# First-phase tiles in another order in memory, three pieces of work moved, and the last sums in fp32

## The chip, the cores and the metric

The kernel runs on one core of a Trainium2 chip. The metric is the device time of one execution in microseconds. Five engines work side by side, each through its own list of instructions in order: TensorE (PE; its weight loads are PEld), VectorE (DVE), ScalarE (ACT), GpSimd (POOL) and SyncE (SP), which here issues all transfers between HBM and on-chip memory. Semaphores tie the lists together. The matrix sums are built in PSUM, all other on-chip data are in SBUF.

## The reference

One layer over 2048 tokens of 1024 channels, in fp32. `gmlp_mixer` and `mlstm_mixer` are two groups of heads on the projections of the normed input; the rest is:

```python
h = rms_norm(x, g_mix)
proj = h @ w_in                                  # 1024 -> u, v, qk, vm, o, gates
gm = gmlp_mixer(u, v, ...)
ml = mlstm_mixer(q, k, vm, ig, fg, o, ...)       # chunks of 128, 4 heads
x = x + concat(gm, ml) @ w_out
h = rms_norm(x, g_ffn)
a, b = split(causal_dwconv(h @ w_up))            # 1024 -> 2 x 2816
x = x + (silu(a) * b) @ w_down
gate = sigmoid(rms_norm(x, g_ple) @ w_ple_gate)
x = x + gate * (p @ w_ple)                       # p: 2048 x 256
out = rms_norm(x, g_final)
```

## The kernel before

The tokens are cut into four blocks of 512. Every product is made of fp32r matmuls on values split into a high and a low part (`whi`/`wlo` for weights, `hh`/`hl` for data): high by high, high by low, low by high, 128 channels at a time. That is why each weight tile, once loaded (`wst`), needs a cast and a subtraction before TensorE can use it: `wsplit` (L102 to L111), with three buffers of each kind in `wpool`.

Phase 1 (`with mx`) runs block by block. `tok_group(0)` to `tok_group(3)` (matmuls in L325 to L327) make the token-major projections with four weight tiles each; then come the q/k tiles, the heads, and `w_out`, whose eight output tiles get the residual added on VectorE (L631) and are stored to HBM as `x1s` (L632). In blocks 1 to 3, `pend[1]`, which is `make_h`, makes the FFN inputs of the block before: it loads `x1s` back (L641), scales with the norm (L204) and stores the `td` tiles (L207). It is called between the layer norm of `gv` (`BN_STATS` L431, GpSimd's power L435, scaling L437) and `tok_group(3)`.

The FFN phase (`with fx`) takes the tokens in two halves. `up_half` makes, for 22 column blocks j, seven products (Winograd's form of a 2x2 block product; L762 to L764) from tiles T (`tt`, split in L680/L681 from `hx` loads) and combined weights (`sw`, split in L686/L687 from `wr`, loaded in L727 to L729). `down_half` sums over the 22 blocks in four double banks of PSUM (L848 to L850), adds the residual (L856), stores `x2s`, and sums squares (L141, L143, `st1` L148/L150). `Steps.run` writes out the matmul steps in order, each with its preparations some steps ahead. The FFN's buffers are slots of one pool, laid over the memory that phase 1 gave free: `w` for weights, `x` for loads, `k` for T tiles, `r` for split weights, `f` and `m`. PSUM is `banks`: four slots of two banks.

Last comes the gate (`Ple`), block by block: for each d of 8 output tiles, 24 matmuls of the gate (`ps`, lines L118, L119, L121 of `mm3`), six of `p @ w_ple` (`pp`), and then L915 (product with the norm `rB`), sigmoid L916, L917 and L918. The norm of a block's input, `n3[b]`, has steps: `st2a` (column sums by matmul L159/L160, the diagonal read out in L163, GpSimd's power), `st2b` (diagonals `dg`, L178) and `st3` (L184/L185 spread the norm over partitions, L187 copies it to SBUF). For block 0, `st2b` and `st3` stand between `steps.run()` and the gate. The last block is gated in two halves a and b of 256 tokens; their final norms go through the same steps, and `emit_half` multiplies (L961; some tiles on GpSimd) and stores (L962) tile by tile.

A scheduler keeps the written order on each engine nearly, but lets ready work of lower rank go between; which slot a tile gets is fixed when the program is built. All transfers are on SP in order, so one that waits holds up all behind it.

Of the kernel before, what the change touches and what calls it, by code (L numbers as in the profile page):

```python
# [41 lines left out]
def trunk_kernel(ctx: ExitStack, tc: tile.TileContext, xT, pT, w_u, w_qk, w_v0, w_v1,  # L42
# [6 lines left out]
    rpool = ctx.enter_context(tc.tile_pool(name="rpool", bufs=2))  # L49
    dram = ctx.enter_context(tc.tile_pool(name="dram", bufs=1, space=bass.MemoryType.DRAM))  # L50
    mx = ExitStack()
    wpool = mx.enter_context(tc.tile_pool(name="wpool", bufs=3))
    hpool = mx.enter_context(tc.tile_pool(name="hpool", bufs=2))
    xpool = mx.enter_context(tc.tile_pool(name="xpool", bufs=2))
    pacc = mx.enter_context(tc.tile_pool(name="pacc", bufs=5, space=PSUM))
    pm = mx.enter_context(tc.tile_pool(name="pm", bufs=3, space=PSUM))
    banks = None
# [20 lines left out]

    col = const.tile([P, NCOL], F32, name="col")
    DMA.dma_start(col, cols)  # L80

    def c1(i):
        return col[:, i:i + 1]
# [15 lines left out]
    one = const.tile([P, 1], F32, name="one")  # L99
    G.memset(one, 1.0)  # L100

    def wsplit(src, n, eng=None, leng=None):  # L102
        st = wpool.tile([P, 1024], F32, tag="wst", name="wst")
        DMA.dma_start(st[:, :n], src)
        hi = wpool.tile([P, 1024], F32R, tag="whi", name="whi")
        if eng is None:
            A.activation(hi[:, :n], st[:, :n], AF.Copy)  # L107
        else:
            eng.tensor_copy(hi[:, :n], st[:, :n])  # L109
        lo = wpool.tile([P, 1024], F32R, tag="wlo", name="wlo")  # L110
        (leng or V).tensor_tensor(lo[:, :n], st[:, :n], hi[:, :n].bitcast(F32), ALU.subtract)  # L111
        return hi, lo
# [19 lines left out]
    class SumSq:  # L132
# [36 lines left out]
        def st2b(self):  # L169
# [7 lines left out]
            for v, dg in zip((rh, rl), self.dg):  # L177
                V.tensor_tensor(dg.rearrange("p (c t) -> p c t", t=128), idb,  # L178
                                v.bitcast(F32).rearrange("p (c o) -> p c o", o=1).broadcast_to([P, nt, 128]),
                                ALU.mult)  # L180

        def st3(self):
            bp = pmt()[:, :self.n]
            PE.matmul(bp, onesr, self.dg[0], start=True, stop=False)  # L184
            PE.matmul(bp, onesr, self.dg[1], start=False, stop=True)  # L185
            self.rB = rpool.tile([P, TB], F32, tag="rB", name="rB")[:, :self.n]
            A.activation(self.rB, bp, AF.Copy)  # L187
# [33 lines left out]
        DMA.dma_start(t[4][:, kk, :], t4)  # L221

    with mx:
        big = mx.enter_context(tc.tile_pool(name="mbig", bufs=1))
        tp = mx.enter_context(tc.tile_pool(name="mtmp", bufs=2))
        sm = mx.enter_context(tc.tile_pool(name="msmall", bufs=2))

# [9 lines left out]
        for k0, k1 in ((0, 1), (1, 2), (2, 4), (4, 6), (6, 8)):  # L237
            xs = xpool.tile([P, 2, TB], F32, tag="xs", name="xs")
            DMA.dma_start(xs[:, 0:k1 - k0, :], xT[0, :, k0:k1, :])
            for k in range(k0, k1):  # L240
                ysplit(xs[:, k - k0, :], C_GMIX, k, h)
                nq.add(xs[:, k - k0, :])
            if k0 == 0:
                w_first = wsplit(w_v0[0], 2 * GW[0], V, V)
        nq.st1()

        ws = big.tile([P, 8, 128], F32, name="ws")
# [51 lines left out]
        for b in range(NB):  # L299
# [135 lines left out]
            G.tensor_tensor(lrs, lrs, mhalf, ALU.pow)  # L435
            for t in range(CPB):
                V.tensor_scalar(gv[:, t, :], gv[:, t, :], mu[:, t, 0:1], lrs[:, t:t + 1], ALU.subtract, ALU.mult)  # L437
            if b:
                pend[1]()
            ps = tok_group(3)  # L440
            for t in range(CPB):
                evac(osig[:, t, 128:512], ps[t][:, 0:384], t)
            for t in range(CPB):
                A.activation(osig[:, t, :], osig[:, t, :], AF.Sigmoid)
            if b == 0:
# [201 lines left out]
    with ExitStack() as fx:  # L647
# [231 lines left out]

        class Ple:  # L880
            def __init__(self, i):
                self.i, self.x, self.h = i, [], []

            def start(self, ds=range(KD)):
                i = self.i
                for d in ds:
                    if i % 2 == 0:
                        x = load2(x2s[i][:, d, :], "xg")
                    else:
                        if d % 2 == 0:  # L890
                            self.xp = pairs(slot("f", "xg"))
                            DMA.dma_start(self.xp, x2s[i][:, d:d + 2, :])
                        x = self.xp[:, d % 2, :]
                    h = slot("k", "hg", F32R)
                    A.activation(h[:, :TB], x, AF.Copy, scale=c1(C_GPLE + d))
                    V.scalar_tensor_tensor(h[:, TB:], x, c1(C_GPLE + d), h[:, :TB].bitcast(F32), ALU.mult, ALU.subtract)
                    self.x.append(x)
                    self.h.append(h)
# [8 lines left out]

            def out_tile(self, d, si, ps):
                lo, hi = self.segs[si]
                pp = acc()[:, :hi - lo]  # L910
                mm3(pp, [(wpe[k][0][:, d * 128:(d + 1) * 128], wpe[k][1][:, d * 128:(d + 1) * 128],
                          self.p[0][:, k * TB + lo:k * TB + hi], self.p[1][:, k * TB + lo:k * TB + hi]) for k in range(2)])
                gs = slot("m", "gs")[:, :hi - lo]
                x = self.x[d][:, lo:hi]
                V.tensor_tensor(gs, ps, n3[self.i].rB[:, lo:hi], ALU.mult)  # L915
                A.activation(gs, gs, AF.Sigmoid)  # L916
                V.tensor_tensor(gs, gs, pp, ALU.mult)  # L917
                V.tensor_tensor(x, x, gs, ALU.add)  # L918
                f = self.fins[si]
                f.add(x)  # L920
                if len(self.segs) > 1:
                    tc.keep_in_program_order(A.activation(x, x, AF.Copy, scale=c1(C_GFIN + d)))
                if d == KD - 1:
                    f.st1()

            def run(self, hooks, cut=(0, TB)):
# [4 lines left out]
                for t in range(KD + len(segs) - 1):  # L931
                    for si, (lo, hi) in enumerate(segs):
                        d = t - si
                        if not 0 <= d < KD:
                            continue
                        w = wpg[d]
                        ps = acc()[:, :hi - lo]
                        mm3(ps, [(w[0][:, k * 128:(k + 1) * 128], w[1][:, k * 128:(k + 1) * 128],
                                  self.h[k][:, lo:hi], self.h[k][:, TB + lo:TB + hi]) for k in range(KD)])
                        if si == 0:  # L940
                            for fn in hooks.get(d, ()):
# [2 lines left out]
                        while len(last) > lag and t > 1:  # L944
                            self.out_tile(*last.pop(0))
                        if len(segs) > 1 and (d, si) == (KD - 2, 1):
                            self.fins[0].st2()
                for o in last:
                    self.out_tile(*o)
                return self.fins  # L950
# [4 lines left out]
                V.scalar_tensor_tensor(x, x, c1(C_GFIN + k), fin.rB, ALU.mult, ALU.mult)  # L955
                DMA.dma_start(out[o.i, :, k, :], x)

        def emit_half(o, fin, lo, hi, pool):
            for k in (pool + tuple(k for k in range(KD) if k not in pool)):
                x = o.x[k][:, lo:hi]  # L960
                (G if k in pool else V).tensor_tensor(x, x, fin.rB, ALU.mult)  # L961
                DMA.dma_start(out[o.i, :, k, lo:hi], x)  # L962

        ple = [Ple(b) for b in range(NB)]

# [33 lines left out]
        ex = {}  # L999
        for b in range(2):  # L1000
            at(1 + b, 5, lambda b=b: n3[b].st2a(r3[:, b, :]))
        up_half(1, ex)

        ex = {}
# [8 lines left out]
        down_half(1, ex)  # L1013
        steps.run()

        n3[0].st2b()
        n3[0].st3()
        wpe.extend(split4(w_pe[k], "r") for k in range(2))
        fin = None
        for b in range(NB):  # L1020
# [14 lines left out]
                continue  # L1035
            cut = (0, TB // 2, TB)
            fa, fb = ple[b].run(hooks, cut)
            fa.st3()
            fb.st2()
            emit_half(ple[b], fa, 0, TB // 2, (0, 4))  # L1040
            fb.st3()
            emit_half(ple[b], fb, TB // 2, TB, (2,))


def _pack(x, p, g_mix, w_in, gm_ln_g, gm_ln_b, gm_ws, gm_bs, ml_conv_w, ml_conv_b, ml_b_i, ml_b_f, ml_norm_g,
# [47 lines left out]
```

## Time and profile before

| | |
|---|---|
| median of 3 runs | 2482.81 us (2481.03 to 2486.6) |
| profiled execution | 2480.78 us |
| its span, first to last instruction | 2479.0 us |
| TensorE busy | 2404.0 us (97%) |
| VectorE, ScalarE, GpSimd busy | 1697.2 (68%), 1066.4 (43%), 53.5 us (2%) |
| mean granted TensorE clock | 0.99 |
| DMA | 324.99 MB, mean 131 GB/s |

The sum of busy time says that TensorE sets the time; what else there is must be found in the places where it waits. A wait is put down to the engine and line that ended it last.

### The profile page before, as it was taken

What the parts mean: (1) busy time and instruction counts of PE and PEld (TensorE: products, weight loads), DVE (VectorE), ACT (ScalarE), POOL (GpSimd) and SP (SyncE); (2) the same over time, 40 slices, a digit from 0 to 9 for tenths busy, and PEclk for the clock granted to TensorE, in tenths of its full rate; (3) what the DMA queues carried; (4) which work ended last, traced back from release to release, by engine and by line L of the source; (5) the groups of instructions that cost most, each with busy time, mean ns of one, the idle gap of its engine ahead of it and who ended that gap; (6) DMA issues with size and microseconds to landing.
All of it is one profiled execution on the core that took longest, in us unless ns stands there. A gap on an engine that the chain in (4) does not pass through costs nothing.

```text
span 2479.0 us, 30740 instructions
## 1 busy us (share of the span) xinstructions
PE 2404.0 (97%) x11596; PEld 2039.9 (82%) x11596; DVE 1697.2 (68%) x2846; ACT 1066.4 (43%) x1707; POOL 53.5 (2%) x62
## 2 busy tenths in 40 slices
PE   8999999999999979999999999999999999989997
PEld 8888987988898858888888887788888888868887
DVE  7687667688656578888776343878877746354666
ACT  3453364256236355444455332444444435332223
POOL 1000000000000000000000000000000000000000
PEclk9999999999999989999999999999999999999999
DMA  6326424472542262344227474322222266550221
GB/s 200 96 69 213 153 85 135 151 241 70 175 132 86 94 238 77 112 157 157 94 91 258 140 250 136 120 77 77 86 93 77 97 212 206 184 189 13 68 69 68
DMA packets 125173, 324.99 MB, mean 131 GB/s; under 512 B 13664, under 2 KB 15840, under 8 KB 125024
## 3 DMA queue, kind: packets, MB, share of 16 engines
q1 hardware_dynamic: 125024, 323.02, 39.3%
q8 instruction: 91, 1.49, 0.2%
q14 instruction: 58, 0.48, 0.1%
HBM read 260.05 MB, written 62.91 MB: 130 GB/s over the span
## 4 chain that ended last, share of the span: by engine, by line
PE 89%; DVE 5%; DMA 3%; ACT 2%; issue 1%; POOL 1%; SPq 0%; DVEq 0%; POOLq 0%; ACTq 0%
PE ub L764 6%; PE ub L763 6%; PE ub L762 6%; PE dn L848 6%; PE dn L849 6%; PE dn L850 6%; PE ua L764 5%; PE ua L762 5%; PE ua L763 5%; PE acc L118 4%; PE acc L119 4%; PE acc L121 4%; PE bank L118 3%; PE bank L119 3%; PE bank L121 3%; PE acc L326 3%
## 5 line engine op out<-in xcount | busy, mean ns | idle before, releaser
L762 PE MATMUL ub<-tt,sw 128*128 128x512 f32 x704 | 276.1, 392 | 13.2 <-ACT tt L680 11.6
L848 PE MATMUL dn<-at,wd 128*128 128x512 f32 x704 | 274.1, 390 | 5.0 <-ACT wd L686 3.3
L763 PE MATMUL ub<-tt,sw 128*128 128x512 f32 x704 | 275.7, 392 | 1.3 <-DVE tt L681 1.3
L764 PE MATMUL ub<-tt,sw 128*128 128x512 f32 x704 | 275.4, 391 | 0.5 <-DVE sw L687 0.5
L849 PE MATMUL dn<-at,wd 128*128 128x512 f32 x704 | 273.9, 389 | 0.0
L850 PE MATMUL dn<-at,wd 128*128 128x512 f32 x704 | 272.5, 389 | 0.0
L686 ACT ACTIVATE sw<-wr 128x1024 fp32r<-128x1024 f32 x132 | 140.3, 1063 | 289.2 <-PE ua L763 257.6
L687 DVE TENSOR_TENSOR wd<-wd 128x1024 fp32r<-128x1024 f32 x88 | 107.9, 1226 | 198.4 <-ACT wd L686 195.1
L687 DVE TENSOR_TENSOR sw<-wr,sw 128x1024 fp32r<-128x1024 f32 x132 | 161.4, 1223 | 75.7 <-ACT sw L686 75.6
L762 PE MATMUL ua<-tt,sw 128*128 128x512 f32 x528 | 205.7, 390 | 0.7 <-ACT sn L768 0.7
L763 PE MATMUL ua<-tt,sw 128*128 128x512 f32 x528 | 205.5, 389 | 0.0
L764 PE MATMUL ua<-tt,sw 128*128 128x512 f32 x528 | 205.4, 389 | 0.0
L111 DVE TENSOR_TENSOR wlo<-wst,whi 128x1024 fp32r<-128x1024 f32 (+2 forms) x144 | 158.6, 1105 | 52.5 <-ACT whi L107 31.2
L326 PE MATMUL acc<-wlo,hh 128*128 128x384 f32 (+1 forms) x512 | 175.6, 343 | 7.8 <-DVE wlo L111 7.8
L325 PE MATMUL acc<-whi,hh 128*128 128x384 f32 (+1 forms) x512 | 172.6, 342 | 8.2 <-DVE whi L109 7.7
L686 ACT ACTIVATE wd<-wd 128x1024 fp32r<-128x1024 f32 x88 | 93.2, 1059 | 192.5 <-PE dn L849 187.4
L327 PE MATMUL acc<-whi,hl 128*128 128x384 f32 (+1 forms) x512 | 174.7, 341 | 0.0
L762 PEld LDWEIGHTS ub<-tt,sw 128*128 128x128 f32 x704 | 133.1, 189 | 42.6 <-ACT tt L680 12.7
L848 PEld LDWEIGHTS dn<-at,wd 128*128 128x128 f32 x704 | 132.1, 188 | 34.5 <-ACT wd L686 4.5
L763 PEld LDWEIGHTS ub<-tt,sw 128*128 128x128 f32 x704 | 133.1, 189 | 30.2 <-DVE tt L681 2.4
L764 PEld LDWEIGHTS ub<-tt,sw 128*128 128x128 f32 x704 | 133.1, 189 | 28.3 <-DVE sw L687 0.9
L850 PEld LDWEIGHTS dn<-at,wd 128*128 128x128 f32 x704 | 132.2, 188 | 27.8 <-DVE wd L687 0.2
(296 smaller groups left out, 5073.9 us busy)
## 6 DMA issues: line engine op xcount, KB each, us to landing
wd<-w_down SPq DMA_DIRECT2D x88, 512.0 KB, 3.6
wr<-w_up SPq DMA_DIRECT2D x44, 512.0 KB, 3.6
wr<-w_up SPq DMA_DIRECT2D x88, 256.0 KB, 4.4
act<-fc SPq DMA_DIRECT2D x44, 512.0 KB, 4.0
wd<-act SPq DMA_DIRECT2D x88, 256.0 KB, 3.9
wst<-w_v SPq DMA_DIRECT2D x48, 384.0 KB, 3.2
wst<-w_qk SPq DMA_DIRECT2D x32, 512.0 KB, 3.6
wst<-w_out SPq DMA_DIRECT2D x32, 512.0 KB, 3.5
```

What stands on the lines that cost most here:

```text
L118: PE.matmul(ps, wh, mh, start=(i == 0), stop=False)
L119: PE.matmul(ps, wh, ml, start=False, stop=False)
L326: PE.matmul(ps[t][:, :n], a_h, rl, start=False, stop=False)
L327: PE.matmul(ps[t][:, :n], a_l, rh, start=False, stop=(k == KD - 1))
L686: A.activation(hi, x, AF.Copy)
L687: V.tensor_tensor(lo, x, hi.bitcast(F32), ALU.subtract)
L762: PE.matmul(ps, hi[:, c], t[:, :HALF], start=first, stop=False, skip_group_check=on)
L763: PE.matmul(ps, hi[:, c], t[:, HALF:], start=False, stop=False, skip_group_check=on)
L764: PE.matmul(ps, lo[:, c], t[:, :HALF], start=False, stop=last, skip_group_check=on)
L848: PE.matmul(ps, hi[:, c], t[:, :HALF], start=(j == 0), stop=False)
L849: PE.matmul(ps, hi[:, c], t[:, HALF:], start=False, stop=False)
L850: PE.matmul(ps, lo[:, c], t[:, :HALF], start=False, stop=(j == NJ - 1))
```

## The change

The diff has six parts. The pools of phase 1 are opened in another order, so that other tiles lie where the FFN's first slots will be. The first weight tile is loaded at the top over ScalarE's queue. `pend[1]()` is called after `tok_group(3)`. `n3[0].st2b` and `st3` become early work of `up_half(1)`, block 3. In the gate, `ps` and `pp` are the two banks of one slot (`gt`). At the end, the two half norms are made by `q1` (plain fp32 matmuls of one column each over the sum of squares) and `q2` (one fp32 diagonal, one fp32 matmul over `ones`), the result is read straight from PSUM by VectorE alone, and two tiles go out in one transfer.

```diff
-    wpool = mx.enter_context(tc.tile_pool(name="wpool", bufs=3))
+    big = mx.enter_context(tc.tile_pool(name="mbig", bufs=1))
     hpool = ...
     xpool = ...
+    wpool = mx.enter_context(tc.tile_pool(name="wpool", bufs=3))
...
     DMA.dma_start(col, cols)
+    w_raw = wpool.tile([P, 1024], F32, tag="wst", name="wst")
+    A.dma_start(w_raw[:, :2 * GW[0]], w_v0[0])
...
+        def q1(self):
+            mp = pmt()
+            nt = self.n // 128
+            for c in range(nt):
+                PE.matmul(mp[:, c:c + 1], self.a[:, c * 128:(c + 1) * 128], one, start=True, stop=True)
+            r = rpool.tile([P, CPB], F32, tag="nr", name="nr")[:, :nt]
+            V.tensor_scalar(r, mp[:, :nt], 1.0 / D, EPS, ALU.mult, ALU.add)
+            G.tensor_tensor(r, r, mhalf[:, :nt], ALU.pow)
+            self.r = r
+        def q2(self):
+            nt = self.n // 128
+            dg = self.t("dgf")
+            V.tensor_tensor(dg..., ident..., self.r..., ALU.mult)
+            bp = pmt()[:, :self.n]
+            PE.matmul(bp, ones, dg, start=True, stop=True)
+            self.rB = bp
...
-                w_first = wsplit(w_v0[0], 2 * GW[0], V, V)
+                w_first = wsplit(None, 2 * GW[0], V, V, w_raw)
...
-            if b:
-                pend[1]()
             ps = tok_group(3)
             for t in range(CPB):
                 evac(osig[:, t, 128:512], ps[t][:, 0:384], t)
+            if b:
+                pend[1]()
...
-                pp = acc()[:, :hi - lo]
+                ps, pp = ps[:, 0, :hi - lo], ps[:, 1, :hi - lo]
...
-                        ps = acc()[:, :hi - lo]
+                        ps = bank2("gt")
...
-                            self.fins[0].st2()
+                            self.fins[0].q1()
...
-        def emit_half(o, fin, lo, hi, pool):
-            for k in (pool + tuple(k for k in range(KD) if k not in pool)):
-                x = o.x[k][:, lo:hi]
-                (G if k in pool else V).tensor_tensor(x, x, fin.rB, ALU.mult)
-                DMA.dma_start(out[o.i, :, k, lo:hi], x)
+        def emit_half(o, fin, lo, hi):
+            for k in range(0, KD, 2):
+                for i in range(2):
+                    x = o.x[k + i][:, lo:hi]
+                    V.tensor_tensor(x, x, fin.rB, ALU.mult)
+                DMA.dma_start(out[o.i, :, k:k + 2, lo:hi], o.xp[k // 2][:, :, lo:hi])
...
+        at(3, 5, n3[0].st2b)
+        at(3, 3, n3[0].st3)
         up_half(1, ex)
...
-        n3[0].st2b()
-        n3[0].st3()
         wpe.extend(split4(w_pe[k], "r") for k in range(2))
...
-            fa.st3()
-            fb.st2()
-            emit_half(ple[b], fa, 0, TB // 2, (0, 4))
-            fb.st3()
-            emit_half(ple[b], fb, TB // 2, TB, (2,))
+            fa.q2()
+            fb.q1()
+            emit_half(ple[b], fa, 0, TB // 2)
+            fb.q2()
+            emit_half(ple[b], fb, TB // 2, TB)
```

VectorE at the end of block 1's `tok_group(2)`, before the change (`xs` is `make_h`'s, `gv` and `mu` the layer norm's, `whi` and `wlo` the weights of `tok_group(3)`):

```order
L204 SCALAR_TENSOR_TENSOR xs<-xs,col,rB 128x512
L432 BN_AGGR mu<-bnst 128x2
L204 SCALAR_TENSOR_TENSOR xs<-xs,col,rB 128x512
L434 TENSOR_SCALAR lrs<-mu 128x4
L109 CAST whi<-wst 128x768
L437 TENSOR_SCALAR gv<-gv,mu,lrs 128x512 x4
L111 TENSOR_TENSOR wlo<-wst,whi 128x768
L109 CAST whi<-wst 128x768
L111 TENSOR_TENSOR wlo<-wst,whi 128x768
```

The same place in the changed kernel (its lines L113 and L115 are the cast and the remainder, L229 is `make_h`, L455 to L461 the layer norm):

```order
L113 CAST whi<-wst 128x768
L455 BN_STATS bnst<-gv 128x6
L115 TENSOR_TENSOR wlo<-wst,whi 128x768
L456 BN_AGGR mu<-bnst 128x2
L455 BN_STATS bnst<-gv 128x6 x2
L456 BN_AGGR mu<-bnst 128x2
L229 SCALAR_TENSOR_TENSOR xs<-xs,col,rB 128x512
L456 BN_AGGR mu<-bnst 128x2
L455 BN_STATS bnst<-gv 128x6
L113 CAST whi<-wst 128x768
L456 BN_AGGR mu<-bnst 128x2
L229 SCALAR_TENSOR_TENSOR xs<-xs,col,rB 128x512
```

The two remaining weight tiles moved up past most of `make_h` and past the `gv` scaling; in the changed kernel the last `wlo` stands directly ahead of L461.

SP at the step from phase 1 to the FFN, before the change (`x1s` the last stores of phase 1, `wr` the first up weights, `hx` the T tiles' data):

```order
L630 DMA xr<-xT 128x512
L632 DMA x1s_81<-xr 128x512 x2
L727 DMA wr<-w_up 128x1024
L728 DMA wr<-w_up 128x512
L729 DMA wr<-w_up 128x512
L675 DMA hx<-td_1_86 128x512 x4
```

And in the changed kernel:

```order
L654 DMA xr<-xT 128x512
L656 DMA x1s_84<-xr 128x512 x2
L751 DMA wr<-w_up 128x1024
L752 DMA wr<-w_up 128x512
L753 DMA wr<-w_up 128x512
L699 DMA hx<-td_1_89 128x512 x4
```

Nothing moved here: the loads stand behind the same two stores.

TensorE at the step from the FFN to the gate, before the change (`dn` are the down sums, `dg` the norm's diagonals, `hg` and `wg` the gate's data and weights):

```order
L848 MATMUL dn<-at,wd 128x512
L849 MATMUL dn<-at,wd 128x512
L850 MATMUL dn<-at,wd 128x512
L184 MATMUL bank<-dg,onesr 128x512
L185 MATMUL bank<-dg,onesr 128x512
L118 MATMUL bank<-hg,wg 128x512
L119 MATMUL bank<-hg,wg 128x512
```

And in the changed kernel:

```order
L872 MATMUL dn<-at,wd 128x512
L873 MATMUL dn<-at,wd 128x512
L874 MATMUL dn<-at,wd 128x512
L122 MATMUL gt<-hg,wg 128x512
L123 MATMUL gt<-hg,wg 128x512
```

The two matmuls of the norm are gone from between the down sums and the gate.

## Rows read from the trace of the kernel before

**Rows 1.** The page, part 1: engine, busy us, share of the span, instructions.
```profile
PE 2404.0 (97%) x11596; PEld 2039.9 (82%) x11596; DVE 1697.2 (68%) x2846; ACT 1066.4 (43%) x1707; POOL 53.5 (2%) x62
```

**Rows 2.** TensorE's waits, whole span: us in total, times, longest us.
```profile
PE bank L184 <- DVE dg L178: 12.0, 2, 9.6
PE ub L762 <- ACT tt L680: 11.6, 2, 9.0
...
PE bank L118 <- DVE junk L163: 1.1, 1, 1.1
```

**Rows 3.** TensorE's timeline, first matmul: start us, us, instruction, idle before, releaser.
```profile
6.73 1.32 PE L325 MATMUL acc<-whi,hh 128*128 128x392 f32 x3 [6.73 <-DVE whi L109]
```

**Rows 4.** VectorE's timeline, 5 to 7 us.
```profile
5.35 0.75 DVE L191 SCALAR_TENSOR_TENSOR hl<-xs,col,hh 128x512 fp32r<-128x512 f32 x1 [3.68 <-ACT hh L190]
6.02 0.56 DVE L109 CAST whi<-wst 128x784 fp32r<-128x784 f32 x1
```

**Rows 5.** TensorE's waits from 284 to 300, 505 to 515, 715 to 735 us.
```profile
PE acc L326 <- DVE wlo L111: 2.2, 1, 2.2
...
PE acc L326 <- DVE wlo L111: 2.3, 1, 2.3
...
PE acc L326 <- DVE wlo L111: 2.7, 1, 2.7
PE acc L325 <- DVE whi L109: 0.8, 1, 0.8
```

**Rows 6.** VectorE's timeline, 293 to 297 us.
```profile
293.64 1.91 DVE L437 TENSOR_SCALAR gv<-gv,mu,lrs 128x512 f32<-128x512 f32 x4 [0.90 <-POOL lrs L435]
295.47 0.95 DVE L111 TENSOR_TENSOR wlo<-wst,whi 128x768 fp32r<-128x768 f32 x1
```

**Rows 7.** SP's timeline, 866 to 873 us (issues).
```profile
866.99 5.76 SPq L632 DMA_DIRECT2D x1s<-xr  x2
872.85 0.38 SPq L727 DMA_DIRECT2D wr<-w_up  x1
```

**Rows 8.** ScalarE's timeline at 878 us.
```profile
877.99 1.06 ACT L686 ACTIVATE sw<-wr 128x1024 fp32r<-128x1024 f32 x1 [23.35 <-DMA wr<-w_up]
```

**Rows 9.** TensorE's timeline, 2215 to 2235 us.
```profile
2215.78 0.39 PE L850 MATMUL dn<-at,wd 128*128 128x512 f32 x1
...
2218.50 0.39 PE L850 MATMUL dn<-at,wd 128*128 128x512 f32 x1
...
2229.63 0.63 PE L118 MATMUL bank<-hg,wg 128*128 128x512 f32 x1
...
2234.75 0.44 PE L118 MATMUL bank<-hg,wg 128*128 128x512 f32 x1
```

**Rows 10.** VectorE's timeline at 2215 us.
```profile
2215.50 3.48 DVE L856 TENSOR_TENSOR xr<-xr,dn 128x1024 f32<-128x1024 f32 x3
```

**Rows 11.** Windows: length, busy PE, PEld, DVE, ACT, POOL, granted clock, DMA share, GB/s.
```profile
2220.00:2230.00 10.00, 1.48 (x3) 1.12 (x4) 9.16 (x13) 4.51 (x8) 0.00 (x0) 0.56 0.98 352
2230.00:2240.00 10.00, 10.00 (x35) 7.99 (x34) 2.77 (x5) 2.97 (x4) 0.00 (x0) 0.76 0.31 126
```

**Rows 12.** TensorE's timeline at 2461 us.
```profile
2461.61 0.40 PE L121 MATMUL bank<-pp,wg 128*128 128x256 f32 x2
```

**Rows 13.** VectorE's timeline, 2457 to 2475 us.
```profile
2457.50 0.42 DVE L915 TENSOR_TENSOR gs<-bank,rB 128x256 f32<-128x256 f32 x1
...
2459.77 0.43 DVE L143 TENSOR_TENSOR sq<-sq 128x256 f32<-128x256 f32 x1
...
2465.11 0.75 DVE L961 TENSOR_TENSOR xg<-xg,rB 128x256 f32<-128x256 f32 x2
...
2471.79 2.96 DVE L961 TENSOR_TENSOR xg<-xg,rB 128x256 f32<-128x256 f32 x7 [1.09 <-ACT rB L187]
```

**Rows 14.** SP's timeline, 2462 to 2479 us (issues).
```profile
2464.07 12.51 SPq L962 DMA_DIRECT2D out<-xg  x16
```

**Rows 15.** TensorE's timeline at 37 us (L363 is an fp32 matmul, four per block).
```profile
37.41 0.95 PE L363 MATMUL pm<-one,gpad 128*128 128x1 f32 x8
```

More of the change, by code (lines that the diff above doesn't have):

```diff
@@ L100, in trunk_kernel, with wsplit @@
     G.memset(one, 1.0)
-    def wsplit(src, n, eng=None, leng=None):
-        st = wpool.tile([P, 1024], F32, tag="wst", name="wst")
-        DMA.dma_start(st[:, :n], src)
+    def wsplit(src, n, eng=None, leng=None, st=None):
+        if st is None:
+            st = wpool.tile([P, 1024], F32, tag="wst", name="wst")
+            DMA.dma_start(st[:, :n], src)
         hi = wpool.tile([P, 1024], F32R, tag="whi", name="whi")
@@ L180, in st2b @@
                                 ALU.mult)
+        def q1(self):
[10 more added lines that the diff above has]
+            dg = self.t("dgf")
+            V.tensor_tensor(dg.rearrange("p (c t) -> p c t", t=128),
+                            ident.rearrange("p (o t) -> p o t", o=1).broadcast_to([P, nt, 128]),
+                            self.r.rearrange("p (c o) -> p c o", o=1).broadcast_to([P, nt, 128]), ALU.mult)
+            bp = pmt()[:, :self.n]
+            PE.matmul(bp, ones, dg, start=True, stop=True)
+            self.rB = bp
         def st3(self):
@@ L223, in trunk_kernel @@
     with mx:
-        big = mx.enter_context(tc.tile_pool(name="mbig", bufs=1))
         tp = mx.enter_context(tc.tile_pool(name="mtmp", bufs=2))
@@ L881, in __init__ @@
             def __init__(self, i):
-                self.i, self.x, self.h = i, [], []
+                self.i, self.x, self.xp, self.h = i, [], [], []
             def start(self, ds=range(KD)):
@@ L890, in start @@
                         if d % 2 == 0:
-                            self.xp = pairs(slot("f", "xg"))
-                            DMA.dma_start(self.xp, x2s[i][:, d:d + 2, :])
-                        x = self.xp[:, d % 2, :]
+                            self.xp.append(pairs(slot("f", "xg")))
+                            DMA.dma_start(self.xp[-1], x2s[i][:, d:d + 2, :])
+                        x = self.xp[-1][:, d % 2, :]
                     h = slot("k", "hg", F32R)
@@ L922, in out_tile @@
                     tc.keep_in_program_order(A.activation(x, x, AF.Copy, scale=c1(C_GFIN + d)))
-                if d == KD - 1:
+                if d == KD - 1 and len(self.segs) == 1:
                     f.st1()
@@ L936, in run @@
                         w = wpg[d]
-                        ps = acc()[:, :hi - lo]
-                        mm3(ps, [(w[0][:, k * 128:(k + 1) * 128], w[1][:, k * 128:(k + 1) * 128],
+                        ps = bank2("gt")
+                        mm3(ps[:, 0, :hi - lo], [(w[0][:, k * 128:(k + 1) * 128], w[1][:, k * 128:(k + 1) * 128],
                                   self.h[k][:, lo:hi], self.h[k][:, TB + lo:TB + hi]) for k in range(KD)])
```

## The prediction, made before the changed kernel had run

> **What bounds the kernel now.** I read the page's engine shares first, then TensorE's waits, then the timelines at the places the change touches. TensorE is busy for 2404.0 of 2479.0 us [rows 1], so nothing that only relieves another engine counts. What can be won are the 75 us in which TensorE waits, and the few places where its clock is low. The list of its waits [rows 2] has four that the change touches: the start; the weight splits of the last token group in blocks 1 to 3; the step from phase 1 to the FFN; and the step from the FFN to the gate. The sum of squares at the very end adds a tail in which TensorE has nothing left to do.
>
> The sum is made against the profiled execution, 2480.78 us (span 2479.0, 1.78 around it). The median of the runs is 2482.81, 2.03 above it; I add that at the end.
>
> **Start.** The first matmul starts at 6.73 us and waits for the cast of the weight tile [rows 3]. That cast stands on VectorE behind `hl` (0.75 us at 5.35) and starts at 6.02 [rows 4]. After the change the weight tile is requested from ScalarE's queue, before SP has issued its other loads, and its cast and its remainder stand ahead of `hl`. The first matmul then needs `hh`, which is ready just as `hl` starts, at 5.35, so at most 6.73 - 5.35 = 1.4 us go. The second and later tiles come over the same queue as before, and a wait for them can take it back. I take -1.0, range 0 to -1.4.
>
> **Phase 1, last token group.** In blocks 1, 2 and 3 the split weights of `tok_group(3)` come late: 2.2, 2.3 and 2.7 + 0.8 us [rows 5], 8.0 in all. The reason is on VectorE [rows 6]: 0.90 us in which it waits for GpSimd's power, then 1.91 us of `gv` scaling, and only at 295.47 the remainder `wlo` for which TensorE stands still until 296.4. Ahead of these stand four scalings of `make_h` (L204). The order of the changed kernel puts the cast and remainder of the third weight tile ahead of `make_h` and among the `BN_STATS`, and those of the fourth ahead of the `gv` scaling. By the same durations, the third remainder is ready at about 288, when TensorE wants it at 296.4 - 2.2 = 294.2; the fourth can start when the first weight tile is used up, two weight tiles earlier than it is wanted. So all of it goes: -8.0. What is late next are the `wlo` of the next `w_qk` tiles, which VectorE now makes after two more L204: these are wanted only in the last third of a tile of 24 matmuls. SP now issues the stores of `make_h` later, between the `w_qk` and `w_u` loads; the loads of the second `w_qk` tile and of `w_u` stood behind such stores before. From below: if one of the two remainders of each block is still late, half stays. Range -4 to -8.
>
> **Layout of the first tiles.** TensorE's last `w_out` matmul ends near 871.7 and the FFN then waits 9.0 us and more [rows 2]. The chain is on SP: the last `x1s` store is issued after VectorE has added the residual (SP's row of two stores, 866.99 and 5.76 long, ends at 872.75), then at 872.85 the first `w_up` load [rows 7], and ScalarE can split it at 877.99, having waited 23.35 us for just that load [rows 8]. The new layout lets the `w_up` tile lie over memory that is free long before. But the order shows both loads and the `hx` loads still behind that last store on SP. What held SP was the store, not the memory. I take 0. From above: if the load could start with the earlier store, at 866.99, 5.9 us would go. From below: the FFN's `k` and `r` slots now lie over the last weight tiles, whose matmuls end at 871.7, while the data to be written there arrive at 877.99; that costs nothing until the load becomes 6 us earlier.
>
> **FFN to gate.** Twelve down matmuls take 2218.50 - 2215.78 = 2.72 us, 0.227 each; the last starts at 2218.50, so the next could at 2218.73. L184 waits 9.6 us [rows 2], and the first gate matmul starts at 2229.63 [rows 9]. It is the order: the norm of gate block 0 (`st2b`, `st3`) stands after `steps.run()`, so L178 is behind the whole residual and squares of the last down block. After the change this norm is made in `up_half(1)`, before the whole of `down_half(1)`, and the gate's matmuls follow the last down matmul in TensorE's order. They need only bank 0 of the down sums to be read, which VectorE has started at 2215.50 [rows 10], three banks in 3.48 us; the second gate tile, 5.4 us later, needs bank 1. So 2229.63 - 2218.73 = 10.9 us go. After the idle stretch the granted clock is 0.56 and then 0.76 of full in the two windows from 2220 to 2240 [rows 11], so part of them passed at 1.2 instead of 2.4 GHz: from 2229.63 to 2234.75 twelve matmuls take 5.12 us against 2.72 before [rows 9], and 2.4 us go with the idle time. The wait of 1.1 us for `junk` [rows 2] is a wait for a PSUM slot that the first `pp` tile needs. With `ps` and `pp` in one slot, `pp` needs none: 1.1 goes. The two matmuls of `st3` are still made, in the up phase, at 2 x 0.23: +0.45. Sum: -10.9 - 2.4 - 1.1 + 0.45 = -14.0. The VectorE work of `st2b` (two casts and two diagonals) lies under up's matmuls; `up_half(0)` already has such a norm at the same steps of its block 7. Added wait: VectorE's product with `rB` waits for the `pp` matmuls of its tile too, since the tile is one; six matmuls, 1.36 us, per tile. Behind it on VectorE are only the same tile's steps, and TensorE wants the slot one tile (5.4 us) later at the earliest. Range -10 (the clock dips all the same and a slot wait stays) to -15.
>
> **End.** The last `pp` matmuls start at 2461.61 [rows 12], and end near 2462.0. From the product with `rB` to the start of the sum, a half tile takes 2459.77 - 2457.50 = 2.27 us [rows 13]: 2462.05 + 2.27 + 0.43 = 2464.75. Half a's diagonal is made just ahead of that sum, its matmul ends near 2465.2. Eight products of half a at 0.75 / 2 = 0.375 each [rows 13] take until 2468.2; `r` of half b (with its GpSimd power) is ready behind them. Then scaling and diagonal, 0.6 (a 128x256 product on VectorE is 0.42), one fp32 matmul of 128x256 over `ones`, 1.0, and eight products, 3.0: 2472.8. The last store is issued at once, since only eight are issued, one per two products. Before, the last products begin at 2471.79, end at 2474.75, and the sixteen stores hold SP until 2464.07 + 12.51 = 2476.6 [rows 14], 2.4 before the end. So 2472.8 + 0.4 + 2.4 = 2475.6, against 2479.0: -3.4. The 1.0 is an estimate: no such matmul is in the trace. A plain fp32 matmul of one column, four in the program, is recorded as eight [rows 15], so two passes; two passes of 256 columns at half clock are about 1. Bounds: 0.3 (one pass, full clock) to 2.3 (twice two). Range -2 to -4.5.
>
> The Trainium skill (FP8 and Floating Point Precision, TensorE Precision Notes) says that true fp32 takes four passes; by that the matmul would be about 2 and the sum 1 us higher. Rows 15 show two records for each; how long one lasts with 256 columns no row shows.
>
> The products of half a and b now read `rB` from PSUM. L915 reads PSUM and takes 0.42, L143 reads SBUF alone and takes 0.43 [rows 13]: no surcharge. The Trainium skill (Perfetto Trace Analysis, Optimizing Scalar/DVE Operations) gives VectorE some 65 ns more on PSUM; for sixteen products that would be 1.0 us on the end. The trace does not agree, so I leave it out.
>
> **Sum.** -1.0 - 8.0 + 0 - 14.0 - 3.4 = -26.4: 2480.78 - 26.4 = 2454.4, and 2.03 more is 2456.4. I forecast 2456. By the ranges of the terms, -28.9 to -16 with the layout at 0, the forecast's own range is 2454 to 2467.
>
> **Rivals.**
> 1. The layout does what its words say, and the FFN starts earlier: 5.9 us less: 2450. For it: ScalarE waits for that one load. Against it: SP's order. 0.07.
> 2. The waits of the last token group come back elsewhere: the L204 move behind the `gv` scaling and the `w_qk` remainders are late instead. All 8.0 stay: 2464. For it: VectorE is the engine waited for at that place. Against it: those remainders are wanted 16 matmuls later than a `wlo` of the token group. 0.10.
> 3. The gate starts early but its first block waits again, for `pp`'s split weights or for `sl` of the last down block: half of the 14 stays, 2463. For it: VectorE is busy for 9.16 of the 10 us from 2220 [rows 11]. Against it: the gate's first three tiles, 16 us, need nothing of it. 0.06.
> 4. Rivals 2 and 3 together with a start and end that give nothing: 2456.4 + 8 + 7 + 4.4 = 2476: no change. 0.04.
> 5. Slower: the shared `ps`/`pp` slot. Three blocks have 8 tiles each and the last 16 half tiles; if every tile held up TensorE by its six `pp` matmuls, that is 24 x 1.36 + 16 x 0.68 = 44 us, 2456 + 44 = 2500. It decides from where VectorE finishes a tile later than one tile's matmuls (5.4 us) after its `pp`. For it: eight `out` products stand in a row on VectorE once per block. Against it: four slots, and a tile's own chain is 2.3 us for a half tile. 0.03.
>
> **How the numbers follow.** Forecast 0.70, rivals 0.07, 0.10, 0.06, 0.04, 0.03. A measurement of this kernel tells about 0.2% (5 us) from no change. Faster by more: 0.70 + 0.07 + 0.10 + 0.06 = 0.93; within: 0.04; slower: 0.03. The range 2448 to 2467 takes in the forecast's own range and rivals 1 to 3; rivals 4 and 5 (0.07) lie outside, and the rest of the 2 in 10 is for terms that I have sized wrongly.
>
> **What would show it.** Right: TensorE's waits for `wlo` in blocks 1 to 3 gone; the first gate matmul 0.2 us behind the last down matmul at full clock; the wait for `tt` at the start of the FFN still near 9; a single short row of eight stores at the end. Wrong: a first `w_up` load issued before the last `x1s` store; new waits of TensorE for `gs` in the gate; a diagonal matmul well over 1 us at the end.

## The result and the profile after

The changed kernel takes 2457.25 us (median of 4 runs, 2455.78 to 2458.61), the kernel before 2481.92, run beside it: ratio 0.9899, 95% interval [0.9882, 0.9916]. The forecast was 2456. The interval lies clear of 1, and the gain is 1.0%. The profiled execution has a span of 2456.8 us against 2479.0, 22.2 less. Where these lie is read by setting the start of the same instruction in both timelines side by side; forecasts are the terms of the prediction, and each row is rounded by itself.

| from ... to | forecast | profile |
|---|---|---|
| start ... first gates (`lf`) of block 1, 245 us | -1.0 | +1.0 |
| ... the same of block 2 | -2.2 | -2.4 |
| ... the same of block 3 | -2.3 | +2.8 |
| ... last residual, 867 us | -3.5 | -5.6 |
| ... first up matmul | 0 | +0.1 |
| ... last down matmul | +0.45 | +1.5 |
| ... first gate matmul | -10.9 | -10.9 |
| ... end | -6.9 | -8.5 |
| sum | -26.4 | -22.2 |

TensorE does the same work in a shorter span: it is busy for 2399.1 us, where it was 2404.0 [rows 1].

TensorE's waits over the whole span, as in [rows 2]. The 9.6 us for the norm's diagonal and the wait for `junk` are gone, as are the four for `wlo` and `whi` of [rows 5]; the wait for `tt` ahead of the FFN is where it was; the 4.0 us at L478 are new.

```profile
PE ub L786 <- ACT tt L704: 11.3, 2, 9.1
...
PE acc L349 <- ACT hh L215: 6.9, 2, 6.1
PE bank L204 <- DVE dgf L200: 5.1, 2, 2.9
PE acc L478 <- ACT cv L502: 4.0, 1, 4.0
```

**The start.** The first matmul starts 0.6 us earlier than before [rows 3], not 1.4: the weights are ready first now, but `hh`, which the prediction had at its old time, comes later. ScalarE waits for the `xs` load of `hh` until 5.36, where it was until 4.59.

```profile
6.13 1.02 PE L349 MATMUL acc<-whi,hh 128*128 128x392 f32 x2 [6.13 <-ACT hh L215]
```

**The new wait in block 2.** Only there `make_h` takes its odd branch, which loads `hs` too and stores five more tiles for each kk. VectorE, where its last kk now stands:

```profile
529.84 1.22 DVE L115 TENSOR_TENSOR wlo<-wst,whi 128x1024 fp32r<-128x1024 f32 x1
537.25 1.42 DVE L229 SCALAR_TENSOR_TENSOR xs<-xs,col,rB 128x512 f32<-128x512 f32 x2 [6.19 <-DMA xs<-x1s]
538.58 1.22 DVE L115 TENSOR_TENSOR wlo<-wst,whi 128x1024 fp32r<-128x1024 f32 x1
```

ScalarE, and TensorE's matmul for which L502 has to free a PSUM slot:

```profile
539.91 1.06 ACT L111 ACTIVATE whi<-wst 128x1024 fp32r<-128x1024 f32 x1 [8.81 <-DVE wlo L115]
540.88 1.43 ACT L502 ACTIVATE cv<-acc,col 128x512 f32<-128x512 f32 x2
```
```profile
541.69 0.50 PE L478 MATMUL acc<-hh,whi 128*128 128x512 f32 x1 [4.00 <-ACT cv L502]
```

The chain runs over four engines: the `x1s` load lands late, VectorE stands 6.19 us for it with a weight remainder `wlo` behind it, ScalarE's next cast needs a weight buffer which that `wlo` gives back, and the q/k tile's evacuation stands behind that cast.

**From phase 1 to the FFN.** SP's issues and the first up matmul, to be held against [rows 7]: the first `w_up` load still comes directly behind the last two `x1s` stores.

```profile
862.72 5.77 SPq L656 DMA_DIRECT2D x1s<-xr  x2
868.58 0.38 SPq L751 DMA_DIRECT2D wr<-w_up  x1
```
```profile
876.47 0.79 PE L786 MATMUL ub<-tt,sw 128*128 128x512 f32 x1 [9.06 <-ACT tt L704]
```

**From the FFN to the gate.** TensorE, and then the window behind it (columns as in [rows 11]): no gap, and the granted clock stays at full, as it is from 2210 to 2220.

```profile
2215.78 0.39 PE L874 MATMUL dn<-at,wd 128*128 128x512 f32 x1
2216.01 0.39 PE L122 MATMUL gt<-hg,wg 128*128 128x512 f32 x1
```
```profile
2220.00:2230.00 10.00, 10.00 (x46) 8.24 (x45) 9.03 (x21) 4.94 (x6) 0.70 (x1) 1.00 0.96 363
```

**The end.** TensorE, VectorE and SP behind the last `pp` matmul, to be held against [rows 12 to 14]:

```profile
2442.53 0.40 PE L125 MATMUL gt<-pp,wg 128*128 128x256 f32 x2
2445.15 0.70 PE L204 MATMUL bank<-dgf,ones 128*128 128x256 f32 x2 [2.22 <-DVE dgf L200]
...
2449.29 1.22 PE L204 MATMUL bank<-dgf,ones 128*128 128x256 f32 x2 [2.90 <-DVE dgf L200]
```
```profile
2446.51 2.40 DVE L986 TENSOR_TENSOR xg<-xg,bank 128x256 f32<-128x256 f32 x7
2448.82 0.42 DVE L200 TENSOR_TENSOR dgf<-ident,nr 128x256 f32<-128x256 f32 x1
2450.55 2.74 DVE L986 TENSOR_TENSOR xg<-xg,bank 128x256 f32<-128x256 f32 x8 [1.31 <-PE bank L204]
```
```profile
2446.95 6.75 SPq L987 DMA_DIRECT2D out<-xg  x8
```

From the last `pp` row to the end it is 14.3 us, where it was 17.4: -3.1. A product with `rB` in PSUM takes 2.40 / 7 = 0.34 us, not more than one with `rB` in SBUF before (2.96 / 7 = 0.42 [rows 13]).

### The profile page after: what moved, and what is told of

Its sections match the earlier page's. It is cut to its first block, busy times and chain, and to the rows that moved or that the text cites. A ratio compares the mean times of both kernels' runs of the same rounds, so it can differ in the third digit from the quotient of the medians.

```text
span 2456.8 us, 30679 instructions
## 1 busy us (share of the span) xinstructions
PE 2399.1 (98%) x11600; PEld 2037.0 (83%) x11600; DVE 1695.4 (69%) x2831; ACT 1063.0 (43%) x1705; POOL 54.1 (2%) x59
## 4 chain that ended last, share of the span: by engine, by line
PE 87%; DVE 5%; DMA 4%; ACT 2%; issue 1%; POOL 1%; SPq 0%; DVEq 0%; ACTq 0%; POOLq 0%
PE ub L787 6%; PE ub L788 6%; PE ub L786 6%; PE dn L872 6%; PE dn L873 6%; PE dn L874 6%; PE ua L787 5%; PE ua L788 5%; PE ua L786 5%; PE acc L122 4%; PE acc L123 4%; PE acc L125 3%; PE gt L122 3%; PE gt L123 3%; PE gt L125 3%; PE acc L349 3%
## 5 line engine op out<-in xcount | busy, mean ns | idle before, releaser
L115 DVE TENSOR_TENSOR wlo<-wst,whi 128x1024 fp32r<-128x1024 f32 (+2 forms) x144 | 158.5, 1104 | 42.4 <-ACT whi L111 22.9
L786 PEld LDWEIGHTS ub<-tt,sw 128*128 128x128 f32 x704 | 132.8, 189 | 42.4 <-ACT tt L704 12.2
```

Of the source, the lines that this page charges most:

```text
L786: PE.matmul(ps, hi[:, c], t[:, :HALF], start=first, stop=False, skip_group_check=on)
```

## The experiments

Each run is compared with the changed kernel's 2457.25 us and, place by place, with its profile. Single executions of phase 1 and of the FFN differ by 2 us and more in either direction, so the reading at the place of the edit counts for more than the whole. The runs were made in four groups: the calls, the norm and the slot; the end, the layout and ScalarE's queue; GpSimd's queue; all of it. The kernel before, run again in each, had medians of 2481.79 to 2486.05 us, so differences between medians of different groups are good to some 4 us only; the ratios are to the kernel before of the same group.

**Call of `make_h`, block 2 alone.**

```diff
+            if b == 2:
+                pend[1]()
             ps = tok_group(3)
...
-            if b:
+            if b in (1, 3):
                 pend[1]()
```

> Changed kernel, but in block 2 alone (where `make_h` also loads `hs` and stores five more tiles) `pend[1]()` is called ahead of `tok_group(3)` again. Theory (VectorE stands 6.2 us behind a late `xs` load with a `wlo` behind it): TensorE's 4.0 us at L478 and 0.5 us at L529 in block 2 go, the 2.3 us of before come back at the last token group; block 2 gains about 2.2, time 2455.1. Rival (the 4.0 us come from the `w_qk` remainders whatever stands there): 4.0 stays and 2.3 is added, 2459.6.

Measured: 2455.41 (2453.22 to 2456.92), ratio 0.9881 [0.9866, 0.9895]. The -1.8 alone decides nothing, but from block 2's first gates to block 3's it takes 3.0 us less than in the changed kernel. The wait at L478 is gone and one of 2.5 us for `wlo` is back, as the theory says. But there is one more that neither expected, on TensorE:

```profile
541.74 0.49 PE L516 MATMUL pm<-qk 128*128 128x128 f32 x2 [2.51 <-ACT qk L508]
```

ScalarE makes that `qk` behind a weight cast that waits for its load, and SP issues the load behind the last stores of `make_h`:

```profile
538.17 1.06 ACT L111 ACTIVATE whi<-wst 128x1024 fp32r<-128x1024 f32 x1 [2.78 <-DMA wst<-w_u]
```
```profile
532.76 0.32 SPq L246 DMA_DIRECT2D td<-hx  x1
533.18 0.40 SPq L108 DMA_DIRECT2D wst<-w_u  x1
```

So the waits that the call's place changes in block 2 come to the same 5 us, and what was won there is clock: the changed kernel has a granted clock of 0.83 from 540 to 550 and from 620 to 630 us, some 1.7 us each, and this run 1.00 throughout the block. The time is the theory's, but the theory's reason (2.2 us less of waiting) is not what happened.

**Call of `make_h`, all blocks** (`pend[1]()` ahead of `tok_group(3)` for every b but 0, the diff undone).

> Changed kernel with `pend[1]()` ahead of `tok_group(3)` in all blocks, as before. Theory: TensorE's 2.2, 2.3 and 2.7 + 0.8 us come back, the 4.0 + 0.5 us at L478/L529 of block 2 go: +3.5, time 2460.8. Rival (the call's place pays its full 8.0 and the 4.0 of block 2 have another cause): +8.0, 2465.3. Rival (it pays nothing): 2457.3.

Measured: 2465.31 (2462.78 to 2468.21), +8.1. TensorE's waits from 240 to 770 us are those of the theory: `wlo` back (and 0.7 us for `whi`), and nothing at L478 or L529:

```profile
PE acc L350 <- DVE wlo L115: 7.3, 3, 2.7
```

By place against the changed kernel: block 1 +6.0, block 2 -4.3, block 3 +5.3. The signs are the theory's, the sizes of blocks 1 and 3 well above the waits. The windows say why (granted clock in the last column but two; the changed kernel has 1.00 in all three). In the first and the last a wait of the list falls; the middle one follows a wait of 2.8 us for `hc` at 408.92 that the changed kernel has too, without the low clock:

```profile
290.00:300.00 10.00, 7.76 (x37) 7.09 (x36) 9.06 (x19) 1.66 (x2) 1.25 (x1) 0.88 0.67 215
410.00:420.00 10.00, 10.00 (x39) 8.00 (x38) 8.70 (x14) 6.23 (x9) 0.00 (x0) 0.83 0.55 171
730.00:740.00 10.00, 8.31 (x40) 8.31 (x41) 5.55 (x8) 1.70 (x3) 0.00 (x0) 0.83 0.49 157
```

Of block 3, 3.4 us are waits and 1.7 clock; of block 1, 2.2 waits and 3.4 clock (1.7 at 290 to 310, 1.7 at 410); the second 1.7 need not come from the call, since its wait stands in both kernels. The time came out at the rival's 2465.3, but its mechanism (a gain of 8.0 and another cause for the wait of block 2) is refuted: that wait goes with the call.

**Norm of the first gate block back behind the FFN.**

```diff
-        at(3, 5, n3[0].st2b)
-        at(3, 3, n3[0].st3)
...
         steps.run()
+        n3[0].st2b()
+        n3[0].st3()
```

> Changed kernel with the first gate norm (`st2b`, `st3`) after all FFN steps again. Theory: the first gate matmul 10.9 us later, 2.4 us of half clock behind it, less 0.45 for the two matmuls in the up phase: +12.9, time 2470.1. Rival (the FFN paid more than the two matmuls, about 1.4 us, for the moved norm): +11.9, 2469.2. Rival (the shared slot and the loads start the gate as early anyway): below +7, 2464.

Measured: 2469.14 (2464.54 to 2471.19), +11.9. TensorE waits again, and the first gate matmul is 10.76 us behind the last down matmul instead of 0.23:

```profile
2214.80 0.39 PE L874 MATMUL dn<-at,wd 128*128 128x512 f32 x1
2224.46 0.76 PE L209 MATMUL bank<-dg,onesr 128*128 128x512 f32 x1 [9.27 <-DVE dg L182]
2225.02 0.74 PE L210 MATMUL bank<-dg,onesr 128*128 128x512 f32 x1
2225.56 0.63 PE L122 MATMUL gt<-hg,wg 128*128 128x512 f32 x1
```

From there to the end it takes 1.5 us more: the slow clock (0.72 granted from 2225.5 to 2230), which the prediction put at 2.4 in the kernel before. At the place that is 10.5 + 1.5 = 12.0. Both first theories fit the time; the third is out. Whether the moved norm costs the FFN more than its two matmuls can't be told: from first up to last down matmul, six executions with it take 1336.7 to 1341.0 us, the two without 1336.3 and 1337.8.

**A slot of its own for `pp`** (`acc()` in place of the second bank of `gt`).

> Changed kernel, but `pp` takes a PSUM slot of its own again. By the prediction's term the 1.1 us wait for the slot of `junk` comes back: 2458.4. By the reading of the two traces (the last gate block also lost 1.8 us of waits) 3.2 us come back: 2460.5. Rival (with `junk` gone from that place nothing waits): 2457.3.

Measured: 2458.16 (2457.52 to 2463.18), +0.9, which alone decides nothing; from first gate matmul to the end +2.3 in the profile. TensorE's waits there show the prediction's 1.1 us, and two more for `gs` in the last block, where each tile of the gate comes as two half tiles:

```profile
PE bank L122 <- DVE junk L167: 1.1, 1, 1.1
PE bank L122 <- DVE gs L941: 1.0, 2, 0.6
```

The 2.3 are a difference: up to the last `pp` matmul it takes 3.1 us more, as the second reading has it, and from there to the end 0.8 less. At the places of these waits the starts move by 1.4 and 1.7 us, which is the 3.1. And the shared slot has a price at the end: VectorE's last product with `rB` waits for the `pp` matmuls in the changed kernel (first; last `pp` row at 2442.53), and in this run (second) only for the gate's, so that it begins ahead of the last `pp` row at 2447.97:

```profile
2442.97 0.42 DVE L939 TENSOR_TENSOR gs<-gt,rB 128x256 f32<-128x256 f32 x1 [1.34 <-PE gt L125]
```
```profile
2447.69 0.42 DVE L939 TENSOR_TENSOR gs<-gt,rB 128x256 f32<-128x256 f32 x1 [1.13 <-PE gt L125]
```

**The end of before** (`st2`/`st3`, `rB` copied, GpSimd and sixteen stores, with all else changed).

> Changed kernel with the end of before (fp32r pairs, `rB` copied to SBUF, three tiles on GpSimd, sixteen stores). Theory: from the last `pp` matmul to the end 17.4 instead of 14.3 us, +3.1, time 2460.4. Rival (the fp32 matmul takes back what the shorter chain gives, and the early end came from the shared slots): 17.4 is not reached, below +1, 2458.

Measured: 2459.77 (2458.3 to 2461.11), +2.5. From the last `pp` row at 2439.11 to the end of the span, 2457.1, it is 18.0 us, +3.7 against the changed kernel and 0.6 more than in the kernel before, whose last product with `rB` begins that much sooner behind the last `pp` matmul. The rival is out. Which of the end's parts (the fp32 matmuls, the products read from PSUM, the stores by twos, GpSimd left out) gives how much was not taken apart.

**Layout, undone** (pools of phase 1 opened in the old order).

> Changed kernel with the pools of phase 1 opened in the old order. Theory (the first `w_up` load stands on SP behind the last `x1s` store either way): no change, 2457.3, and TensorE's wait for `tt` at the first up matmul still 9.0. Rival (the new order freed the memory and what was won went elsewhere): the wait grows by 1 to 6, 2458 to 2463.

Measured: 2456.53 (2454.31 to 2457.13), ratio 0.9884 [0.9867, 0.9901]: no change. From the last residual to the first up matmul 8.8 us, against 9.0.

**First loads of the FFN on ScalarE's queue**, with the new layout and with the old.

```diff
+                q = A if (self.s, j) == (0, 0) else DMA
-                DMA.dma_start(self.w[:, 0:2, :], ...)
+                q.dma_start(self.w[:, 0:2, :], ...)
...
-            ... load2(tds[s][prod][:, kk, :], "hx") ...
+            ... load2(tds[s][prod][:, kk, :], "hx", A if (s, prod) == (0, 1) else DMA) ...
```

> Changed kernel, but the first three `w_up` loads and the first four `hx` loads are issued from ScalarE's queue, where nothing stands ahead of them after 850.4 us. Theory (only SP's order kept the new layout from paying): they are issued about 17 us earlier; the first up matmul waits only for the second `tt` cast, whose memory the last `w_out` matmul frees at 867.3, and starts near 869.7 instead of 876.5: -6.5, 2450.8. Rival (the loads are not what the first up matmul needs last): 2457.3.

> The same loads from ScalarE's queue, with the pools of phase 1 in the old order. Theory (there the `w_up` tile lies over memory that phase 1 uses until its last matmuls): the load is issued near 867.3 instead of 868.6, -1.3, 2456.0. Rival (the queue alone does it, the layout nothing): as with the new layout, 2450.8.

Measured: 2464.60 (2463.87 to 2465.8) and 2461.79 (2459.25 to 2464.92), both slower, also against the run before them with the old layout and all loads on SP (2456.53, same group), and the first up matmul 12.3 and 12.2 us behind the last residual. Every theory missed. ScalarE with the new layout, and SP beside it:

```profile
849.95 0.36 ACTq L752 DMA_DIRECT2D wr<-w_up  x1
855.40 0.36 ACTq L753 DMA_DIRECT2D wr<-w_up  x1
859.96 0.36 ACTq L754 DMA_DIRECT2D wr<-w_up  x1
866.06 6.32 ACTq L699 DMA_DIRECT2D hx<-td  x4
```
```profile
855.40 0.33 SPq L654 DMA_DIRECT2D xr<-xT  x1
...
859.95 0.33 SPq L654 DMA_DIRECT2D xr<-xT  x1
```

The first load goes out 17 us before the residual, but it and the next two go out in step with SP's `xr` loads (SP issues one at 849.95 too). The trace has the semaphores: each of these loads, and the `xr` load beside it, waits on the one that tells of the landing of an `x1s` store from SP, and is issued within 0.03 us of it (849.93, 855.38 and 859.93). So the loads were still tied to phase 1's transfers, and now ScalarE stood at them, with the `tt` casts behind. That the semaphore alone holds them was read from the trace and not tested by itself.

**The same loads on GpSimd's queue**, whose transfers have semaphores of their own (`G` for `A` in the diff above), new layout and old.

> Changed kernel (new layout), with the first three `w_up` loads and the first four `hx` loads issued from GpSimd's queue, which has no other transfers and shares no semaphore with SP's. Theory (only the loads' place behind the last stores kept the FFN from starting early): they are issued well before the last residual, ScalarE casts the first `sw` as soon as the last `w_out` matmuls free its memory, and the first up matmul follows the last residual by about 2.5 us instead of 9.0: -6.5, 2450.8. Rival (the `hx` data or the T tiles are still late, through the thirteen loads on SP): between 0 and -3, 2454 to 2457. Rival (loads from GpSimd land slower than from SP): 2457 or more.

> The same loads from GpSimd's queue, with the pools of phase 1 in the old order. Theory (with ScalarE's queue the first load was issued about 17 us before the last residual in the new layout and 12.7 us before it in the old, so both leave time enough): as with the new layout, within 1 us, 2450 to 2452. Rival (the new layout is what lets the FFN start early): the first up matmul 9 us behind the last residual, 2457.

Measured: 2459.16 (2457.02 to 2461.36) and 2459.12 (2455.72 to 2459.73). With the new layout GpSimd issues the first load at 831.25, with the old one at 853.24: the layout does free that memory, 22 us earlier. And the first up matmul comes 1.6 and 0.8 us behind the last residual. But the second doesn't follow. TensorE and VectorE, new layout:

```profile
868.93 0.51 PE L787 MATMUL ub<-tt,sw 128*128 128x512 f32 x1 [1.67 <-ACT tt L704]
877.35 0.79 PE L788 MATMUL ub<-tt,sw 128*128 128x512 f32 x1 [7.92 <-DVE tt L705]
```
```profile
876.00 0.69 DVE L765 TENSOR_TENSOR wr<-wr 128x512 f32<-128x512 f32 x1 [5.79 <-DMA wr<-w_up]
876.61 0.68 DVE L705 TENSOR_TENSOR tt<-hx,tt 128x512 fp32r<-128x512 f32 x1
```

On VectorE the remainder of the first T tile stands behind work that waits for the second weight set, and that set is loaded on SP behind the last stores. The wait has only moved one matmul on: the second is 10 us behind the residual with the new layout and 8.7 with the old, where it was 10.7 in the changed kernel. The times miss both theories. They fit the last rival's 2457 or more, but not its reason: GpSimd's loads had landed by 842.09 in the new layout, long before TensorE needed them.

**All of it**: block 2's early call, and `w_up` of j = 0 and 1 and eight `hx` loads on GpSimd's queue, new layout and old.

```diff
-                q = G if (self.s, j) == (0, 0) else DMA
+                q = G if self.s == 0 and j < 2 else DMA
...
-            ... "hx", G if (s, prod) == (0, 1) else DMA) ...
+            ... "hx", G if s == 0 and prod < 3 else DMA) ...
```

> Changed kernel with block 2's `pend[1]()` ahead of `tok_group(3)`, and the `w_up` loads of j = 0 and 1 and the first eight `hx` loads on GpSimd's queue. Theory (with four `hx` loads and one weight set on that queue the second up matmul stood 7.9 us behind VectorE, which waited for the weight set of j = 1, still loaded on SP): the up matmuls start 1.6 us behind the last residual and run on, -6.5 to -7.5; with block 2's 2.2 that is 2447.5 to 2448.5, and 1 to 3 less if the slow clock after the idle stretch goes too. Rival (the up phase then waits for the `hx` loads left on SP): 2452 to 2455.

> The same with the pools of phase 1 in the old order. Theory (there the first `sw` and `tt` casts do not lie over the last weight tiles, and the loads are early enough): the first up matmul 0.8 us behind the last residual instead of 1.6, time within 1.5 us of the run with the new layout. Rival (the new layout is needed for an early start once the loads are free of SP): 4 us or more slower than it.

Measured: 2451.05 (2448.85 to 2453.51), ratio 0.9876 [0.9861, 0.9890], and 2449.54 (2448.53 to 2451.02), ratio 0.9869 [0.9852, 0.9885]. The old layout is not slower. Both lie 1 to 4 us above the theory's 2447.5 to 2448.5, since the up matmuls do not run on: the second still waits 2.5 us for VectorE. The second up matmul in the two, new and old:

```profile
872.21 0.79 PE L790 MATMUL ub<-tt,sw 128*128 128x512 f32 x1 [2.50 <-DVE tt L707]
```
```profile
871.04 0.79 PE L790 MATMUL ub<-tt,sw 128*128 128x512 f32 x1 [2.50 <-DVE tt L707]
```

The first stands 0.8 us behind the last residual in both, the second 3.8, instead of 9.0 and 10.7 in the changed kernel. From last residual to last down matmul they take 1340.4 and 1340.5 us; with all loads on SP it was 1345.2 to 1350.2 (8 executions). With the new layout GpSimd's loads go out from 830.52 on, and VectorE then waits for phase 1's own `xr`:

```profile
849.59 0.69 DVE L657 TENSOR_TENSOR xr<-xr,acc 128x512 f32<-128x512 f32 x1 [8.96 <-DMA xr<-xT]
```

That memory free early makes the transfers early, and these compete with the last tiles of phase 1: two `x1s` stores issued from 835.53 on land after 7.6 and 9.0 us, where the same two (issued from 836.42 on) take 2.1 each in the changed kernel. In the old layout the loads start at 854.07, soon enough.

## Why the prediction was right, and where its sum was not

The time came out 1.3 us above the forecast, but by terms that missed in both directions.

- **Start, -1.0.** At 76 us the changed kernel is 0.6 ahead of before in its first profile, and 0.3 to 1.8 (median 1.1) over it and the twelve others that have this start. The size is right; the prediction did not reckon with a later `hh`. That the table has +1.0 at 245 us comes from block 0's end: between 170 and 200 us nine of the thirteen have one or two stretches with a granted clock of 0.83, and the single profile of before has none; at 245 us the thirteen differ among each other by 5 us. Whether that is chance or belongs to the change can't be told, and the start was not undone by itself.
- **Last token group, -8.0.** The step that failed is "so all of it goes". The profile's net of the three blocks is -5.3, in the lower part of the range: the four waits went, and rival 2 (given 0.10) came true in one block of three. The prediction looked behind the moved call only for the `wlo` of the next tiles, and held these to be wanted late; it did not follow `make_h`'s own load, which in the odd branch comes late, nor the weight buffer that ties ScalarE's next cast to that `wlo`. Another error hid a part of this one: each wait was priced by its length, while in block 3 the kernel before also lost clock behind it, so that 5.6 us went there for waits of 3.5. Undoing the call costs 6.0 and 5.3 us in blocks 1 and 3 for waits of 2.2 and 3.4, with stretches of slow clock in both; but in the kernel before block 1 had 1.00 at that place, and 2.4 went for its 2.2. Block 3 before the change (columns as in [rows 11]); after it the clock is 1.00:

```profile
730.00:740.00 10.00, 10.00 (x49) 9.61 (x48) 3.45 (x4) 4.51 (x7) 0.00 (x0) 0.85 0.62 208
```

- **Layout, 0.** Right, and for the reason given: SP's order, not the memory. The bound of 5.9 us from above was about right too: with the loads off SP, and the second weight set with them, 6.4 to 6.9 us go up to the second matmul and 5 to 10 up to the last down matmul, in either layout.
- **FFN to gate.** -10.9 measured to the tenth, and the norm's return costs +11.9. The slow clock behind it, put at 2.4, came back as 1.5. The shared slot's term was too small: it wins 3.1 in the gate instead of 1.1, since the waits for `gs` in the last block were not read as slot waits, though they stand in the kernel before too. The feared wait of `rB`'s product (rival 5) does not hold up TensorE, which waits for nothing in the gate; but it delays VectorE, and at the end, where the prediction put it at nothing, it costs 0.8. The waits for `gs` before the change:

```profile
PE bank L118 <- DVE gs L917: 1.0, 2, 0.6
```

- **End, -3.4.** -3.1 in the profile, 3.7 by undoing it, 2.5 in the medians. The fp32 matmul estimated at 1.0 took 1.26 us from its start to the first product that needed it, at a granted clock of 0.50; the one of half a, at 1.00, took 0.74. The estimate was near it by luck: at 0.227 us for 512 columns, its two passes of 256 columns make 0.45 at half clock and not 1. Between the two levels of 1.2 and 2.4 GHz the time differs by 0.52 us; by the same 0.227, two passes would differ by 0.23 and four by 0.45. The Trainium skill (FP8 and Floating Point Precision, TensorE Precision Notes) has four passes for true fp32. The trace is nearer to that than to two, so the two records of [rows 15] need not be two passes. The Trainium skill (Perfetto Trace Analysis, Optimizing Scalar/DVE Operations) gives VectorE some 65 ns more on PSUM. The trace shows nothing of it: 0.34 us for a product from PSUM against 0.42 from SBUF.

So the right total rests in part on luck. In the profile all up to the first up matmul gave 4.8 us less than forecast, the FFN 1.1 less, the gate and the end 1.6 more: 22.2 in place of 26.4. The medians differ by 24.7, since the changed kernel's profiled execution lies above its median and that of before below. Not settled is why the same wait brings a slow stretch in one execution and not in another (below), and with it a part of block 2's 3 us.

## What to carry to other kernels

Follow a moved piece of work with its loads: ask for each of its instructions what it waits for at the new place, and what stands behind it on that engine and, through buffers given back late, on the next. Freeing memory earlier pays only if the load into it is not queued behind something later; find out what the issue waits for (queue, semaphore, then memory), and for all the loads that the first steps need, not for the first one alone. Price a wait of TensorE by the time up to the next common mark in two traces, not by its length: a stretch of slow clock beside it added 1.7 us to a wait of 2.2 here.

## What was not expected of the hardware

The granted clock is not a function of the wait alone. In the ten microseconds from 620, with the same wait of 2.6 us (L558 for `hc`) and the same busy time of 7.37 us, the changed kernel, first, was given 0.83 and the run with all calls early 1.00, and started 28 and 35 matmuls:

```profile
620.00:630.00 10.00, 7.37 (x28) 5.59 (x27) 7.89 (x17) 4.54 (x9) 1.37 (x1) 0.83 0.19 54
```
```profile
620.00:630.00 10.00, 7.37 (x35) 5.56 (x34) 9.10 (x25) 4.44 (x13) 1.38 (x1) 1.00 0.37 107
```

Seven matmuls of 0.227 are 1.6 us. Between its start and its last tile, phase 1 had none to five such stretches from execution to execution; a part of the 2 to 7 us by which runs of one kernel differ is of this size.
